# Pairs of chunks in seven block products over all 16 k-tiles, with half of the combined tiles kept in DRAM

## The chip, the cores and the metric

The kernel runs on one core of one Trainium2 chip. The metric is the device time of one execution in microseconds (us); lower is better. TensorE (PE) multiplies, VectorE (DVE), ScalarE (ACT) and GpSimd (POOL) do the element-wise work, SyncE (SP) issues nearly all DMA transfers, in its own order. PSUM is TensorE's output memory, eight banks.

## The reference

Two layers of a hybrid trunk over 640 tokens (128 context, 512 latent) with 2,048 features, in fp32. Each layer normalises, modulates, projects, mixes, gates and projects back:

```python
for l in range(DEPTH):                                    # DEPTH = 2
    shift, scale, gate = modulation(c, ada_w[l], ada_b[l])
    h = rms_norm(x, norm_g[l]) * (1.0 + scale) + shift
    y = even_mixer(h, ...) if l % 2 == 0 else odd_mixer(h, ...)
    x = x + gate * (y @ w_out[l])
y = rms_norm(x, final_norm_g)

def odd_mixer(h, w_in, ...):
    qc, kc, vc, u, v, gp = split_cols(h @ w_in, ODD_SPLITS)   # 48 column blocks of 128 features, and 16 gates
    yc = neighbourhood_attention(qc, kc, vc, ...)             # ctx_attention for context tokens
    yd = spatial_gating(u, v, gnorm, ws, b)
    return jnp.concatenate([yc, yd], -1) * jax.nn.silu(gp)
```

`h @ w_in` and `y @ w_out` are nearly all of the arithmetic. The even layer has its own mixer, which this change leaves as it is.

## The kernel before

Activations lie feature-major: 16 k-tiles of 128 features by 640 token columns, and two leading columns that carry the modulation's shift. A weight chunk is 2,048 input features by 128 output features, so 16 k-tiles by 128. To keep fp32 precision every operand is split into a high part in the fast format fp32r (`ah`, `whi`) and the rest (`al`, `wlo`), and each product is three matmuls: high x high, high weight x low activation, low weight x high activation. The 640 columns are two halves of 320 (322 with the shift columns), one PSUM bank each.

Weights come raw from DRAM (`wraw` for four k-tiles of one chunk, `rs` for block products), ACT makes `whi`, and POOL subtracts it from the raw tile to make `wlo`. `whi` and `wlo` are rings of five blocks of 128x512 (`RING`), filled from a list of jobs (`wstart`, `wpump`).

Most chunks of the first output projection, the odd layer and the second output projection go in pairs (`spair`). Of the 16 k-tiles of two chunks and two column halves, k-tiles 0 to 7 are multiplied plainly and 8 to 15 as a 2 x 2 block product with seven multiplications instead of eight (Strassen's scheme in Winograd's form). With `NS = 4` a block is four k-tiles: weight blocks A11, A12, A21, A22 (`A1x` the first chunk, `x1` k-tiles 8 to 11), their combinations S1 to S4 (DVE block sums, `rs<-rs`), and four combinations of activation tiles. Three of these are kept split in `eh`, `el`; the fourth, T3, overwrites the second column half of k-tiles 8 to 11 in `ah`, `al`. `fold` makes them at a layer's start, and `unfold` reads the overwritten halves back from DRAM (`bh_dram`, `bl_dram`) at its end. Around a fold the chunks run as `kpair`: two chunks k-tile by k-tile, each tile replaced by the next layer's once both have read it.

The raw results of the products meet in PSUM: `sums` holds a copy on ACT, DVE adds it to another bank, and the bank's evacuation follows.

Order: while the program is written out, a planner (`Pace`) estimates when every engine is done with what, and emits an engine's next instruction when it expects its inputs; the engines then run these fixed lists and wait on semaphores. The modulation's matrix-vector work (`adas`, tensor reductions on DVE) fills gaps as the lowest task (`ada_task`). DMA transfers are put on SP's queue when the planner expects them to be free to go. `self.now` is the planner's time.

In the profile L371 is the matmul in `mm`, L376 the transpose in `tr`, L1199 the modulation matmul, L403 the DMA in `dma`, and L205 the one helper line through which DVE, ACT and POOL instructions are recorded, so groups are told apart by tile names.

Of the kernel before, what the change touches and what calls it, by code (L numbers as in the profile page):

```python
# [9 lines left out]
F32 = mybir.dt.float32  # L10
# [16 lines left out]
SPILL, YSP, KEEP = "x1T_dram", "yT_dram", ("bh_dram", "bl_dram")  # L27
# [4 lines left out]
NS = 4  # L32
SJ = KT - 2 * NS
# [5 lines left out]
LAST, STEPS = ((*range(12, 16), *a, *b) for a, b in ((range(8), range(8, 12)), ((*range(4), *range(8, 12)), range(4, 8))))  # L39
LEAD, FIRST = 2, 8  # L40


class Pace:
# [19 lines left out]
    def span(self, ap):  # L63

        if ap.space == bass.MemoryType.DRAM and ap.name not in (SPILL, YSP, *KEEP):
# [165 lines left out]
class Trunk:  # L231
# [9 lines left out]
    def __init__(self, tc, d, es):  # L241
# [11 lines left out]
        self.folded = self.quiet = False  # L253
        self.room = self.rooms[0]
# [11 lines left out]
        self.Y = self.P([128, KT, T], "Y")  # L266
# [29 lines left out]
        self.part = {k: self.P([128, n, 2], "part" + k) for k, n in (("g0", 16), ("1", 32), ("g1", 16))}  # L296


# [12 lines left out]
    def s(self, tag, w=1):  # L311
        return self.t(self.sml, [128, w], tag, bufs=6)
# [74 lines left out]
    cap, hold = 2.0, 99.0  # L387
    lags2, cap2 = (8.0, 6.0, 4.0, 1.0, 0.4), 2.0
    rooms, calms, lags = (0.3, 1.5), (4.0, 2.0), (3.0, 3.0, 2.0, 1.0, 0.4)
# [35 lines left out]
    def until(self, *aps):  # L425
        while self.left(*aps) > 0.05:
# [27 lines left out]
    def tick(self, n=1):  # L454
        self.dmas()
        for _ in range(3):
# [10 lines left out]
        for _ in range(4):  # L467
            if self.low and not (self.quiet and self.tasks) and self.low[0] <= self.now and self.pace.t["v"] <= self.now + self.room:
                try:
                    self.low[0] = max(self.low[0], self.now - 2.0) + (next(self.low[1]) or 0.0)  # L470
                except StopIteration:
                    self.low = None

# [37 lines left out]
    def wstart(self, chunks, acts):  # L511
# [6 lines left out]

        def unit(c, k, r=0):
            self.jobs.append(("split", (c, k, r), len(self.plain), 4, chunks[c][1]))  # L520
            self.plain.append((c, k))
# [4 lines left out]
        last = None  # L526
        self.both = {c for kind, x in acts if kind == "h" for c in x[:2]}
        for kind, x in acts:
# [14 lines left out]
            elif kind == "s":  # L543
                last = self.strassen_jobs(*x, last, unit)

    @staticmethod
    def steps(c1, c2):

        a, b = [[(c, k, 0) for k in range(0, SJ, 4)] for c in (c1, c2)]
        names = lambda *x: [(c1, f) for f in x]  # L550
        return [*names("A11"), *a[:1], *names("A12"), *a[1:], *names("S1", "S2", "S4"), *b[:1], *names("S3"), *b[1:], *names("A22")]

    def strassen_jobs(self, c1, c2, last, unit):
        n, J = NS, self.jobs
        piece = lambda i, m=1: self.rs[:, 128 * n * i : 128 * n * (i + m)]
        load = lambda i, c: ("load", lambda: (piece(i, 2), self.chunks[c][0][:, SJ : SJ + 2 * n, :]))
        add = lambda o, a, b, op: ("add", lambda: (piece(o), piece(a), piece(b)), op)
        if last is None:
            J += [load(0, c1), load(2, c2)]
        else:  # L560
            J.insert(last[0], load(0, c1))
            J.insert(last[1] + 1, load(2, c2))

        at = {"A11": 0, "A12": 1, "S1": 4, "S2": 2, "S4": 1, "S3": 4, "A22": 3}
        after = {
            "A12": [add(4, 2, 3, ALU.add), add(2, 4, 0, ALU.subtract)],
            "S1": [add(1, 1, 2, ALU.subtract)],
            "S2": [add(4, 3, 2, ALU.subtract)],
        }
        for c, f, *r in self.steps(c1, c2):  # L570
            if r:
                unit(c, f)
                continue
            J.append(("split", (c1, f), lambda i=at[f]: piece(i), n, 128))
            J += after.get(f, [])
            if f == "S4":
                done = len(J)
        return done, len(J)
# [4 lines left out]
    def wload(self):  # L583

        c, k = self.plain[self.nraw]
        a = 512 * (self.nraw % 4)
        w = self.chunks[c][0]
        m = w.shape[2]
        self.dma(self.wraws[:, a : a + 4 * m].rearrange("p (a b) -> p a b", b=m), w[:, k : k + 4, :])
# [8 lines left out]
    def wpump(self, force=False):  # L598

        nc, pc = self.nc, self.pace  # L600
        while self.nraw < len(self.plain) and self.nraw < self.nsplit + 4:
# [3 lines left out]
        job = self.jobs[self.job]  # L605
        if job[0] == "load":
            dst, src = job[1]()
            self.dma(dst.rearrange("p (a b) -> p a b", b=128), src)
# [6 lines left out]
            or pc.ready(e, outs, ins) > self.now + lag  # L615
        )
        if job[0] == "add":
            o, a, b = job[1]()
            if not force and late("v", [pc.span(o)], [pc.span(a), pc.span(b)]):
                return False  # L620
            nc.vector.tensor_tensor(o, a, b, job[2])
# [5 lines left out]
        if isinstance(raw, int):  # L627
            m = self.chunks[key[0]][0].shape[2]
            at = 512 * (raw % 4)
# [28 lines left out]
        eng = nc.vector if key[0] in self.both and self.nsplit % 2 else nc.gpsimd  # L658
        eng.tensor_tensor(lo, raw, hi.bitcast(F32), ALU.subtract)
        self.parts[key] = hl  # L660
# [5 lines left out]
    def wget(self, key):  # L666
        while key not in self.parts:
            assert self.wpump(force=True), ("no room for weights", key, self.live)
        return self.parts[key]
# [65 lines left out]
    def kpair(self, c1, c2, order, ready=None, free=None):  # L735
# [7 lines left out]
        for i, (c, k) in enumerate(steps):  # L743
# [3 lines left out]
            if self.folded and SJ <= k < SJ + NS:  # L747
                self.need("unfold")
# [7 lines left out]
            if k == order[-1]:  # L756
                self.chunks[c][4](*banks[c])
# [4 lines left out]
    def hpair(self, c1, c2, after):  # L762

        for half in range(2):
            if half:
                self.need("unfold")
# [14 lines left out]
    def spair(self, c1, c2):  # L781
# [1725 lines left out]
```

## Time and profile before

| | us |
|---|---|
| median of 3 runs (2157.09 to 2159.94) | 2157.79 |
| span of the profiled execution (2.1 below the median; no time of its own beside it is given) | 2155.7 |
| busy: PE / DVE / ACT / POOL | 2099.9 / 1320.2 / 907.2 / 944.9 |
| moved by DMA | 303 MB, 141 GB/s on average |

A group in the profile names engine, operation, output tile <- input tiles with their shape and count, then busy time, mean ns of one, idle time of the engine just before them and what ended it. In a row of waits stand the total, the number and the longest. In an engine's timeline a bracket holds the idle time ahead of an instruction.

### The profile page before, as it was taken

To read this page: it belongs to the slowest core of one execution; us is meant where nothing else is said; L and a number is where in the kernel's file an instruction comes from. 1 tells how busy PE (TensorE), PEld (TensorE's weight loads), DVE (VectorE), ACT (ScalarE), POOL (GpSimd) and SP (SyncE) were. 2 spreads that over 40 slices of the span, in tenths; PEclk is the share of its full clock that TensorE was granted. 3 is DMA by queue.
4 is the path that set the end of the run, shared out by engine and by line. 5 is a ranking of instruction groups with operands and counts; after the bars stand their busy time and mean duration, and the time that the engine had idled before them with its cause. 6 is when DMAs were issued, how large, how long until landed. Compare 5 with 4: busy or idle time off the path is not lost.

```text
span 2155.7 us, 38542 instructions
## 1 busy us (share of the span) xinstructions
PE 2099.9 (97%) x14326; PEld 2029.6 (94%) x14326; DVE 1320.2 (61%) x3190; ACT 907.2 (42%) x1962; POOL 944.9 (44%) x731
## 2 busy tenths in 40 slices
PE   7999999999999999999999999999999999999997
PEld 4789999999989999999999999999999999999996
DVE  1337787777777665889767887874344443354335
ACT  4435444343343444433464333444444453343333
POOL 3433333233223222566544455544444445536663
PEclk9999999999999999999999999999999999999998
DMA  9934433346435332577634345532222232233325
GB/s 374 365 136 153 133 103 105 105 126 192 124 98 165 128 123 81 193 226 220 212 99 127 119 139 163 185 103 79 89 78 78 88 134 80 80 109 122 105 93 193
DMA packets 161372, 303.08 MB, mean 141 GB/s; under 512 B 17376, under 2 KB 54048, under 8 KB 161184
## 3 DMA queue, kind: packets, MB, share of 16 engines
q1 hardware_dynamic: 159712, 299.06, 42.8%
q8 instruction: 112, 1.84, 0.3%
q10 hardware_dynamic: 1472, 1.56, 0.2%
q14 instruction: 76, 0.62, 0.1%
HBM read 278.52 MB, written 19.42 MB: 138 GB/s over the span
## 4 chain that ended last, share of the span: by engine, by line
PE 85%; DVE 5%; DMA 4%; issue 2%; POOL 2%; ACT 2%; SPq 0%; ACTq 0%; DVEq 0%; POOLq 0%
PE bank L371 82%; PE bank L376 2%; PE bank L1199 1%; DVE Y L205 1%; POOL wlo L205 1%; DMA rs<-w_out 1%; DVE arena L205 1%; DVE adas L205 1%; DMA adas<-ada 1%; ACT arena L205 1%; DVE bank L205 0%; ACT whi L205 0%; SPq L403 0%; DVE rs L205 0%; DMA crow<-crow 0%
## 5 line engine op out<-in xcount | busy, mean ns | idle before, releaser
L371 PE MATMUL bank<-acth,whi 128*128 128x320 f32 (+2 forms) x3592 | 1106.6, 318 | 18.2 <-DVE sums L205 8.8
L371 PE MATMUL bank<-acth,wlo 128*128 128x320 f32 (+2 forms) x3592 | 1078.6, 310 | 0.0
L371 PE MATMUL bank<-actl,whi 128*128 128x320 f32 (+2 forms) x3592 | 1077.3, 310 | 0.0
L205 POOL TENSOR_TENSOR wlo<-wraw,whi 128x512 fp32r<-128x512 f32 x375 | 504.2, 1348 | 724.2 <-ACT whi L205 634.0
L371 PEld LDWEIGHTS bank<-acth,whi 128*128 128x128 f32 (+1 forms) x3592 | 668.8, 189 | 35.5 <-DVE sums L205 10.3
L371 PEld LDWEIGHTS bank<-actl,whi 128*128 128x128 f32 (+1 forms) x3592 | 668.9, 189 | 1.5
L371 PEld LDWEIGHTS bank<-acth,wlo 128*128 128x128 f32 (+1 forms) x3592 | 668.4, 189 | 0.0
L205 POOL TENSOR_TENSOR wlo<-rs,whi 128x512 fp32r<-128x512 f32 x259 | 352.1, 1369 | 308.4 <-ACT whi L205 293.0
L205 ACT ACTIVATE whi<-wraw 128x512 fp32r<-128x512 f32 x383 | 237.0, 625 | 251.2 <-PE bank L371 116.0
L205 DVE TENSOR_TENSOR rs<-rs 128x512 f32<-128x512 f32 x148 | 155.2, 1050 | 134.0 <-DMA rs<-w_odd 57.8
L205 DVE CUSTOM_DVE_ANT_0 adas<-adas,bank,partg 128x256 bf16<-128x256 f32 (+1 forms) x320 | 178.6, 558 | 12.7 <-ACT bank L205 3.5
L205 ACT ACTIVATE whi<-rs 128x512 fp32r<-128x512 f32 x259 | 156.4, 621 | 27.3 <-PE bank L371 14.7
L205 DVE CUSTOM_DVE_ANT_0 adas<-adas,bank,part 128x512 bf16<-128x512 f32 x192 | 143.0, 745 | 9.7 <-ACT bank L205 3.6
L205 DVE TENSOR_TENSOR bank<-bank,sums 128x320 f32<-128x320 f32 (+1 forms) x148 | 72.4, 497 | 120.9 <-PE bank L371 120.2
L371 PE MATMUL bank<-eh,whi 128*128 128x322 f32 (+1 forms) x444 | 139.9, 315 | 0.0
L371 PE MATMUL bank<-el,whi 128*128 128x322 f32 (+1 forms) x444 | 137.6, 310 | 0.0
L371 PE MATMUL bank<-eh,wlo 128*128 128x322 f32 (+1 forms) x444 | 137.6, 310 | 0.0
L205 ACT ACTIVATE arena<-Y 128x320 f32<-128x320 f32 (+1 forms) x76 | 38.8, 512 | 172.7 <-DVE Y L205 152.8
L205 ACT ACTIVATE arena<-arena,bc 128x128 f32<-128x128 f32 (+4 forms) x171 | 84.9, 520 | 58.0 <-DVE arena L205 55.8
L205 ACT ACTIVATE bc<-bank 128x2 f32<-128x2 f32 (+1 forms) x101 | 17.2, 170 | 201.1 <-DVE arena L205 120.9
L205 POOL TENSOR_TENSOR arena<-arena 128x320 f32<-128x320 f32 x58 | 53.6, 924 | 103.8 <-ACT arena L205 103.2
L205 ACT ACTIVATE Y<-bank 128x128 f32<-128x128 f32 (+5 forms) x130 | 50.9, 410 | 110.4 <-PE bank L371 85.7
(159 smaller groups left out, 2215.5 us busy)
## 6 DMA issues: line engine op xcount, KB each, us to landing
wraw<-w_even SPq DMA_DIRECT2D x176, 256.0 KB, 3.2
adas<-ada_g SPq DMA_DIRECT2D x128, 256.0 KB, 3.7
adas<-ada SPq DMA_DIRECT2D x128, 256.0 KB, 3.6
wraw<-w_odd SPq DMA_DIRECT2D x124, 256.0 KB, 3.1
rs<-w_odd SPq DMA_DIRECT2D x50, 512.0 KB, 4.1
wraw<-w_out SPq DMA_DIRECT2D x88, 256.0 KB, 3.3
Y<-ada SPq DMA_DIRECT2D x37, 512.0 KB, 6.9
more<-ada SPq DMA_DIRECT2D x27, 512.0 KB, 7.1
```

The source lines that it names most:

```text
L205: return f(*args, **kw)
L371: self.nc.tensor.matmul(out, lhsT, rhs, start=start, stop=stop, **kw)
L376: self.nc.tensor.transpose(out, in_, self.ident[:k, :k])
L1199: nc.tensor.matmul(o, c, w[:, j, :], start=(q == 0), stop=(q == 3))
```

## The change

`NS` becomes 8: a full pair takes all 16 k-tiles in seven block products of eight tiles, as two halves of four (`h` = 0 near, 1 far), and has no plain part. Nine of the 37 pairs keep the form before (`ns = NR = 4`), with blocks of four k-tiles and a plain part: all six of the first output projection, one in the odd layer and the first two of the second projection (`SHORT`).

```diff
-NS = 4
-SJ = KT - 2 * NS
+NS = 8
+NR = 4
+SHORT = 6, 2
 ...
+    def steps(c1, c2, ns):
+        if ns == NS:
+            todo = "A11' A11 S1' S1 A12 A12' S4 S2' S2 S4' S3 S3' A22' A22".split()
+            return [(c1, f.rstrip("'"), int(f[-1] == "'")) for f in todo]
 ...
-        at = {"A11": 0, "A12": 1, "S1": 4, "S2": 2, "S4": 1, "S3": 4, "A22": 3}
+        at = {"11": 0, "21": 1, "22": 2, "12": 3}
+            sums = {
+                "S1": ("21", "21", "22", ALU.add),
+                "S2": ("11", "21", "11", ALU.subtract),
+                "S4": ("12", "12", "11", ALU.subtract),
+                "S3": ("21", "22", "11", ALU.subtract),
+            }
 ...
+        dve = self.nsplit % 2 if key[0] in self.both else self.share and pc.t["g"] > max(pc.t["v"], self.now) + self.share
+        if dve and self.share:
+            self.lows.append((key, hl[0], lambda: (sub(nc.vector), self.parts.update({key: hl})), raw))
 ...
+    def far_load(self, i, f, shift):
+        o = 0 if shift else 2
+        self.dma(self.slots[i][:, :, o:].bitcast(U32), self.far[:, i, f, :, o:].bitcast(U32))
 ...
+            for i in range(4):
+                three(view(b), hi[:, i, :], lo[:, i, :], x(4 * key[2] + i), st and i == 0, i == 3)
+                if again is not None and key[2]:
+                    self.far_load(i, again, shift)
 ...
+                yield from sub(j1, j2, j1)
+                yield from sub(j2, m2, j2)
+                yield from split(self.t3[:, i], self.stage, j2)
+                yield from sub(m2, m2, j1)
+                yield from split(out(0), j2, j1)
+                yield from sub(m1, m1, m2)
+                yield from split(out(1), self.stage, m2)
+                yield from split(out(2), j1, m1)
 ...
+                for n, x in enumerate((self.ah, self.al)):
+                    self.dma(x[:, i, CW:].bitcast(U32), self.t3[:, i, n, :].bitcast(U32))
 ...
-        for j in range(SJ, SJ + NS):
+        for j in range(self.deep):
             for x, y in zip((self.ah, self.al), self.keep):
-                self.dma(x[:, j, CW:].bitcast(U32), y[:, j - SJ, :].bitcast(U32))
+                self.dma(x[:, j, CW:].bitcast(U32), y[:, j, :].bitcast(U32))
 ...
-                    pairs((KT - 4) // 2)
+                    pairs((KT - 4) // 2, SHORT[l], f"us{l}")
```

What comes with it:

- The combined tiles of the near half stay in `eh`, `el`. Those of the far half are made on POOL by `far` (eight subtractions of 320 columns for each of four tile pairs), stored to DRAM (`far_dram`), and streamed into four slots of a tile `tail`. A slot is loaded with the next combination when its product has read it.
- To make room, `Y`, the store of mixer outputs, has 12 tiles of its own instead of 16; four more lie in `tail` while it holds no slots, two borrow the modulation's buffer `adas` (`GHOSTS`), and parts of the attention's and the gating unit's results pass through DRAM (`hT_dram`, `yT_dram`).
- T3 is made for all eight near and far tiles at the fold, stored (`t3_dram`) and read into `ah`, `al` (`third`); `unfold` returns up to eight column halves instead of four.
- Raw weight blocks are 128x1024 and use `rs` and `wraw` together. A low part goes to DVE where the planner sees POOL more than 1 us behind (`share`).
- Bank evacuations and pieces of `fold` are handed out when the planner expects their data (`defer`, `settle`) and no longer stand in an engine's list ahead of it.
- The modulation for the odd layer is fetched as scale, then shift, and the scaling of its input runs as a task (`scales`).

SP's queue beside two attention heads of the odd layer. `rs` and `wraw` are raw weights, `o_nv`, `na_bias` and the caches belong to the attention, `tail<-far_dram` is a load of a far slot, `ada_g` a modulation weight. Before:

```order
L403 DMA rs_7718<-w_odd 128x1024
L403 DMA wraw<-w_odd 128x512 x2
L403 DMA Y<-na_bias 128x1024
L403 DMA Y<-cache_na_kT 128x128
L403 DMA Y<-cache_na_v 128x128
L403 DMA o_nv<-Y 128x128
```

Now:

```order
L428 DMA tail_10968<-far_dram 128x644 x4
L428 DMA adas<-ada_g 128x2x256
L428 DMA hT_dram<-Y 128x640
L428 DMA o_nv<-Y 128x128
L428 DMA Y<-na_bias 128x1024
L428 DMA Y<-cache_na_kT 128x128
L428 DMA Y<-cache_na_v 128x128
L428 DMA tail_10968<-far_dram 128x644 x4
L428 DMA wraw<-w_odd 128x1024
```

The far loads, four at a time, have come into the one queue between weights, modulation weights and the attention's own transfers.

POOL over one pair of the second output projection. `wlo` is a low part of the weights, `arena<-arena` the square of a new output. Before:

```order
L205 TENSOR_TENSOR wlo<-rs_7718,whi 128x512
L205 TENSOR_TENSOR wlo<-wraw,whi 128x512
L205 TENSOR_TENSOR wlo<-rs_7718,whi 128x512
L205 TENSOR_TENSOR wlo<-wraw,whi 128x512
L205 TENSOR_TENSOR arena_16766<-arena_16766 128x320 x2
L205 TENSOR_TENSOR wlo<-rs_7718,whi 128x512 x3
L205 TENSOR_TENSOR wlo<-wraw,whi 128x512
L205 TENSOR_TENSOR arena_16766<-arena_16766 128x320
L205 TENSOR_TENSOR wlo<-rs_7718,whi 128x512
L205 TENSOR_TENSOR wlo<-wraw,whi 128x512
L205 TENSOR_TENSOR wlo<-rs_7718,whi 128x512
L205 TENSOR_TENSOR arena_16766<-arena_16766 128x320
```

Now:

```order
L208 TENSOR_TENSOR arena_16792<-arena_16792 128x320 x2
L208 TENSOR_TENSOR wlo<-rs_7767,whi 128x512 x4
L208 TENSOR_TENSOR wlo<-wraw,whi 128x512 x2
L208 TENSOR_TENSOR arena_16792<-arena_16792 128x320
L208 TENSOR_TENSOR wlo<-wraw,whi 128x512 x2
L208 TENSOR_TENSOR wlo<-rs_7767,whi 128x512
L208 TENSOR_TENSOR arena_16792<-arena_16792 128x320
L208 TENSOR_TENSOR wlo<-rs_7767,whi 128x512 x3
L208 TENSOR_TENSOR wlo<-wraw,whi 128x512
```

The pair had 11 low parts between its four squares; it now has 13 on POOL, and a fourteenth on DVE.

More of the change, by code (lines that the diff above doesn't have):

```diff
@@ new lines, in later, with one, two, three_ @@
+        def later(c, gen):
+            self.evq.append([self.now, gen, c])
+        def one(xa, x):
+            yield from self.until(x)
+            plus(full(xa), x)
+            yield from ev(c1, xa, None)
+            self.drop(xa)
+        def two(x, v):
+            yield from self.until(x)
+            plus(x, half(v))
+        def three_(xb, x):
+            yield from self.until(x)
+            plus(half(xb), x)
+            yield from ev(c1, None, half(xb))
+            self.drop(xb)
@@ new lines, in four @@
+        def four(ya, v, x):
+            yield from self.until(x)
+            plus(full(ya), x)
+            plus(half(v), half(x))
+            yield from ev(c2, ya, None)
+            yield
+            yield from ev(c2, None, half(v))
+            self.drop(ya, v)
+        t = take()
+        xa = xb = v = ya = None
+        steps = self.steps(c1, c2, ns)
+        for n, key in enumerate(steps):
+            c, f, h = key
+            last = f not in [x[1] for x in steps[n + 1 :]]
+            if isinstance(f, int):
+                if c == c1:
+                    xa, xb = xa or take(), xb or take()
+                    plain(key, xa, xb)
+                else:
+                    ya = ya or take()
+                    plain(key, ya, v)
+                if c == c1 and f > NS:
+                    later(c1, one(xa, x))
@@ L865, in spair @@
-                ev1(xa, None)
-                self.drop(xa)
-                v = take()
-                product(v, full, f, tt(0))
+                if v is None:
+                    v = take()
+                    self.need("Tf" if ns == NS else "Tn")
+                product(v, full, key, tt(0), 1)
             elif f == "S2":
-                product(t, full, f, tt(1))
-                x = copy(half(t))
-                plus(x, half(v))
+                product(t, full, key, tt(1), 2)
+                if last:
+                    x = copy(half(t))
+                    later(c1, two(x, v))
@@ L898, in fold @@
+                if last:
+                    later(c2, four(ya, v, x))
+    def fold(self, ready, used, far_used, shift=None, yt=None):
+        nc = self.nc
+        yt = yt or (lambda k: self.Y[:, k, :])
+        self.flags -= {"Tn", "Tf", "T30", "T31"}
+        if not far_used:
+            self.flags |= {f"{ready}f{k}" for i in range(NR, NS) for k in (i, NS + i)}
         one, two = slice(0, HT), slice(HT, T)
         left = [2, 2]
+        staged = []
+        pair = lambda x: x.rearrange("p (a b) -> p a b", b=HT)
@@ L952, in fold @@
+        if shift is not None:
+            self.spawn(shifts())
         for w in range(2):
             self.spawn(work(w))
+        if far_used:
+            self.spawn(far(0))
+            self.spawn(far(1))
+        self.spawn(third())
     def split2(self, h, l, x, scale=1.0):
@@ L1686, in evac, with end @@
             G = self.G[l]
-            y = self.Y[:, f, :]
+            y = self.yt(f) if l else self.Y[:, f, :]
+            if l == 0 and f in GHOSTS:
+                y = box["x"]
+            def end(c):
+                yield from self.until(y[:, c], self.sq)
+                square(y, c)
+                if c.start and spill is not None:
+                    self.dma(spill[:, f, :], y)
+                    self.flags.add(f"sp{f}")
+            x = box["x"]
             if pa is not None:
-                x = box["x"]
+                self.need(f"y{l}f{f}")
                 nc.vector.scalar_tensor_tensor(
```

685 lines of the change are left out of this document (464 added, 221 removed).

## The prediction

> **What bounds the kernel now.** I read the page's head first, then busy time by stage, then who makes TensorE wait, then single instructions in the stages that the change rewrites.
>
> The head of the page, engine and busy time:
>
> ```profile
> span 2155.7 us, 38542 instructions
> PE 2099.9 (97%) x14326; PEld 2029.6 (94%) x14326; DVE 1320.2 (61%) x3190; ACT 907.2 (42%) x1962; POOL 944.9 (44%) x731
> L371 PE MATMUL bank<-acth,whi 128*128 128x320 f32 (+2 forms) x3592 | 1106.6, 318 | 18.2 <-DVE sums L205 8.8
> ```
>
> TensorE is busy 97% of the span, but matmuls overlap: 318 ns is the life of one, not what one costs. The price is the distance of two starts, from TensorE's timeline (start, duration, instruction); the two rows are 28 matmuls apart in an unbroken run:
>
> ```profile
> 1299.75 0.31 PE L371 MATMUL bank<-acth,whi 128*128 128x320 f32 x1
> ...
> 1303.89 0.31 PE L371 MATMUL bank<-el,whi 128*128 128x322 f32 x1
> ```
>
> (1303.89 - 1299.75) / 28 = 0.148 us per matmul of 320 or 322 columns. By stage (first number the length, then busy time and count of PE, PEld, DVE, ACT and POOL, the granted clock, DMA share, GB/s):
>
> ```profile
> 900.00:1050.00 150.00, 142.20 (x958) 140.92 (x958) 128.82 (x313) 49.46 (x102) 97.66 (x82) 1.00 0.72 225
> 1050.00:1200.00 150.00, 147.00 (x985) 145.74 (x985) 101.00 (x271) 79.44 (x186) 68.21 (x53) 0.99 0.45 139
> 1200.00:1400.00 200.00, 200.00 (x1378) 199.93 (x1377) 163.85 (x459) 77.31 (x162) 105.36 (x78) 1.00 0.47 148
> 1400.00:1760.00 360.00, 359.03 (x2385) 345.79 (x2385) 172.42 (x500) 157.01 (x366) 158.83 (x122) 1.00 0.27 85
> 1760.00:1930.00 170.00, 168.71 (x1140) 168.30 (x1140) 67.96 (x109) 71.98 (x146) 83.92 (x63) 1.00 0.32 105
> 1930.00:2156.00 226.00, 210.53 (x1421) 209.19 (x1419) 101.45 (x180) 84.09 (x165) 136.16 (x112) 0.97 0.38 127
> ```
>
> The first output projection is 900 to 1050, the odd layer about 1050 to 1930, the second output projection and the end come last. From 1050 to 1930 TensorE idles 5.3 us of 880 and its clock is full: there a matmul less is 0.148 us less, as long as its operands arrive. DVE, ACT and POOL have room in that stage; DVE is nearest to full at 1200 to 1400 with 164 of 200 us.
>
> **The change, part by part.** *Matmuls removed.* A pair of chunks costs 96 + 7 x 4 x 3 = 180 matmuls before (eight plain k-tiles in two chunks and two halves, three matmuls each, and seven products of four tiles), and 7 x 8 x 3 = 168 now. Of the 37 pairs nine keep the short form (six in the first output projection, one in the odd layer, two in the second projection), so 28 x 12 = 336 go, all of them after 1050 us. The built order agrees: 13,534 matmul rows before, 13,198 now, no other kind changed in sum. 336 x 0.148 = **49.7 us** less, the gain if TensorE stays fed.
>
> *Splitting and adding weights.* A full pair splits 14 half blocks in place of 11 and adds 8 in place of 4. The order has 726 high parts on ACT in place of 642 (84 x 0.62 = 52 us on an engine that is 42% busy: nothing); low parts 623 on POOL and 112 on DVE in place of 643 and 8; block sums 260 on DVE in place of 148; and 64 new subtractions of 320 columns on POOL. What these cost depends on one another, as the timelines show (POOL at two places, then DVE at the same):
>
> ```profile
> 1811.30 1.29 POOL L205 TENSOR_TENSOR wlo<-wraw,whi 128x512 fp32r<-128x512 f32 x1 [1.61 <-DVE bank L205]
> 1816.93 4.30 POOL L205 TENSOR_TENSOR wlo<-rs,whi 128x512 fp32r<-128x512 f32 x3 [4.34 <-ACT whi L205]
> ...
> 963.39 0.88 POOL L205 TENSOR_TENSOR arena<-arena 128x320 f32<-128x320 f32 x1 [0.60 <-ACT arena L205]
> 968.72 1.84 POOL L205 TENSOR_TENSOR wlo<-wraw,whi 128x512 fp32r<-128x512 f32 x1 [0.70 <-ACT whi L205]
> ...
> 1816.45 0.69 DVE L205 TENSOR_TENSOR rs<-rs 128x512 f32<-128x512 f32 x1
> 1818.32 1.76 DVE L205 TENSOR_TENSOR rs<-rs 128x512 f32<-128x512 f32 x1 [1.19 <-POOL wlo L205]
> ...
> 968.71 2.40 DVE L205 TENSOR_TENSOR rs<-rs 128x512 f32<-128x512 f32 x2 [1.35 <-DMA rs<-w_out]
> ```
>
> A block sum takes 0.69 us where POOL has only just begun, and 1.76 us inside POOL's run of 4.30: it stood for 1.07 us. POOL's own 1.29 becomes 1.84 at 968.72, beside two block sums that began at 968.71. So DVE's two-input work and POOL's take turns, and their times add up against TensorE's.
>
> In the second projection the order has, over the 660 matmuls of its full pairs (97.7 us), 50 low parts and 16 squares on POOL, and 28 sums and 6 low parts on DVE: 50 x 1.29 + 16 x 0.88 + 34 x 0.69 = 64.5 + 14.1 + 23.5 = 102 us. That is 4 us more than TensorE needs. Bounds: 0, if low parts made ahead and the short pairs' slack cover it; 18, if each of the 34 also holds POOL up by 0.55 (1.84 against 1.29) on top. I take **+4**, nearest to the free durations. For the odd layer I need the length of its full pairs, by the first and the last combined-tile products there (duration in ns least/median/most, first and last start):
>
> ```profile
> L371 PE MATMUL bank<-eh,whi x20: 307/311/314, 1157.5 to 1189.4; 128*128 128x322 f32 x20
> L371 PE MATMUL bank<-eh,whi x4: 309/312/314, 1890.2 to 1891.6; 128*128 128x322 f32 x4
> ```
>
> From the second pair's start (1157.5 + 26.6 for a pair - 10.7 for the 72 matmuls ahead of this product = 1173) to 1892 it is 719 us for 24 pairs, and 719 - 288 x 0.148 = 676 now. POOL's and DVE's turns there are 278 x 1.29 + 247 x 0.69 = 529 us: 78%, hidden, 0.
>
> The Trainium skill speaks against the change here ("SBUF — State Buffer", section "Who interferes with whom"): a DVE instruction with two SBUF inputs and a GpSimd instruction that reads SBUF exclude each other for the whole instruction, and the second is blocked, not slowed. The trace agrees (1.76 against 0.69). By a bandwidth that is merely shared the term would be 0; by the lock it is the 4 above or more.
>
> *The far tiles.* Each full pair streams three sets of four combined tiles (330 KB each) from DRAM into four slots: a slot is loaded again when its product has read it, and used 58, 58 and 46 matmuls later: 8.6, 8.6 and 6.8 us. The trace has no such load. The nearest: 320 KB reads, 512 KB and 256 KB weights over the whole run, then in the busiest steady stretch, then 320 KB in the saturated first 90 us (KB each, median us from issue to landing):
>
> ```profile
> rs<-w_out SPq DMA_DIRECT2D x24, 512.0 KB, 4.3
> wraw<-w_out SPq DMA_DIRECT2D x88, 256.0 KB, 3.3
> ```
> ```profile
> wraw<-w_out SPq DMA_DIRECT2D x23, 256.0 KB, 4.3
> rs<-w_out SPq DMA_DIRECT2D x9, 512.0 KB, 5.5
> arena<-xT SPq DMA_DIRECT2D x10, 320.0 KB, 3.8
> ```
> ```profile
> GB/s 10 294 174 418 419 417 397 391 404 408 411 402 380 401 413 408 400 406 409 396 407 403 403 406 402 402 324 338 355 412 339 383 409 412 374 392 334 349 273 340
> Y<-xT SPq DMA_DIRECT2D x13, 320.0 KB, 7.6
> ```
>
> A full pair moves 2.1 MB of weights and 12 x 0.33 = 4.0 MB of tiles in 168 x 0.148 = 24.9 us: 244 GB/s, near the 225 of 900 to 1050, against some 400 at full rate. One load lands in 3.8 us; the fourth of a set queues 3 x (0.33/0.4 - 0.44) = 1.2 us behind the others, 5.0; at this load the weights land 1.0 to 1.2 us later than on average, so 6.2. Against 6.8 that holds on medians, but only by 0.6 us. Bounds: 0, and 28 us if every pair loses 1 us in its tight gap. I take a late load of 0.5 us in a third of the 28 tight gaps, **+5**.
>
> *SP's queue* now carries 1,497 transfers in place of 1,064, in order, and weight loads stand at its head until POOL has read their buffer:
>
> ```profile
> SPq L403 <- POOL wlo L205: 1267.7, 402, 13.9
> SPq L403 <- DVE partg L205: 88.7, 55, 6.1
> ```
>
> 402 waits of 3.2 us on average cost nothing so far, since only weights for later lay behind them. A far tile behind such a wait is late by it; the bounds above hold this too.
>
> *Hand-overs.* Before the first full pair of a layer the four far tile pairs are combined on POOL (32 x 0.88 = 28 us per layer), stored and loaded; the fourth combination of all tiles (T3) now goes through DRAM; at a layer's end eight column halves come back instead of four. In the odd layer the far combination has one k-pair and the short pair to finish: 192 + 180 + 24 matmuls, 58.6 us, for 28 us of far work and 8 + 11 + 4 low parts, 30 us if all are POOL's. That just fits. The returning halves are needed some 36 matmuls (5.3 us) after the last pair, against these rows:
>
> ```profile
> acth<-bh_dram SPq DMA_DIRECT2D x12, 160.0 KB, 4.4
> actl<-bl_dram SPq DMA_DIRECT2D x12, 160.0 KB, 4.8
> ```
>
> Bounds 0 and 12 (three hand-overs of one landing, 4 us each); I take **+4**.
>
> *The rest.* The first projection keeps its short pairs; of its 7.8 idle us most is this:
>
> ```profile
> PE bank L371 <- DVE sums L205: 7.8, 5, 2.3
> ```
>
> Evictions are now handed out when their data is there, which may win up to 4 of these; the modulation work on DVE is partly drawn forward and may cost as much. I take 0. The modulation fill otherwise stays in the gaps DVE has.
>
> Sum: -49.7 + 4 + 5 + 4 = -36.7 on a span of 2155.7. The profile gives no time of its own around that span; the median of the runs is 2157.8, 2.1 above it, and I keep this distance: 2157.8 - 36.7 = **2121**.
>
> **Rivals.** *All is hidden:* the four terms are 0 as the order was laid for it; 2108, or 2104 with the 4 us of the first projection. For it: 5.3 idle us in 880. Against it: the 102 us in 98.
>
> *The shared turns bind in every full pair:* this is the lock named above, as a result of its own. The rows' means instead of the free durations:
>
> ```profile
> L205 POOL TENSOR_TENSOR wlo<-rs,whi 128x512 fp32r<-128x512 f32 x259 | 352.1, 1369 | 308.4 <-ACT whi L205 293.0
> L205 DVE TENSOR_TENSOR rs<-rs 128x512 f32<-128x512 f32 x148 | 155.2, 1050 | 134.0 <-DMA rs<-w_odd 57.8
> ```
>
> 50 x 1.37 + 16 x 0.92 + 34 x 1.05 = 119 against 97.7: +21 in the second projection; the odd layer's 278 x 1.37 + 247 x 1.05 = 640 of 676 us would just hold. With +21 in place of +4 the time is 2138, and 2145 if the odd layer loses 1%.
>
> *Far tiles come late in every pair: slower.* If DMA saturates at 1200 to 1400, where the modulation weights are fetched beside them, a 320 KB load lands in 7.6 us and the fourth in 8.8: 0.2 + 0.2 + 2.0 = 2.4 us lost per pair, 67 us; 2121 - 5 + 67 = 2183. It decides from 1.5 us lost per pair ((49.7 - 8) / 28). For it: SP's waits of 3.2 us. Against it: 244 of 400 GB/s.
>
> *Nothing gained:* about half of that lateness, 40 us, and 2156.
>
> **Chances.** Forecast (2112 to 2132) 0.50; all hidden 0.15; turns bind 0.18; nothing gained 0.06; slower 0.11. The range goes from 2104 to 2150: it leaves out the slower case and most of "nothing gained". The likeliest case alone has 2112 to 2132. Faster by over 0.2% (4.3 us, about what a measurement can tell): 0.50 + 0.15 + 0.18 and a third of the sixth case, 0.85; within 0.2%, 0.04; slower, 0.11.
>
> **What would show it.** Right: 13,198 matmuls of the same 0.148 us; from 1050 on TensorE idles some 13 us more; POOL and DVE together are full in the second projection, DVE's sums there at 1.0 us or more. Far loads land in 4 to 6 us; waits of TensorE for DMA on the tail tile add to about 5. Wrong: TensorE waits for tail loads in every pair, or for low parts through the whole odd layer, or DMA near its full share there.

## The result, and the profile after

The changed kernel is slower: 2185.9 us median (2180.7 to 2190.5, four runs) against 2157.7 for the kernel before, a ratio of 1.013 (95% interval 1.0112 to 1.0147). The forecast was 2121, in a range of 2104 to 2150. It was to become 37 us faster and became 28 us slower.

The head of the page after, engine and busy time, and its row for the far tiles' loads (KB each, median us to landing):

```profile
span 2185.5 us, 39032 instructions
PE 2083.0 (95%) x13990; PEld 1992.6 (91%) x13990; DVE 1537.5 (70%) x3389; ACT 959.0 (44%) x2084; POOL 1021.9 (47%) x775
...
tail<-far_dram SPq DMA_DIRECT2D x288, 322.0 KB, 4.8
```

14,326 - 13,990 = 336 matmuls are gone, as forecast, and in an unbroken run they still start 0.148 us apart. DVE is busy 217 us more. By stage, in the columns of the table of before:

```profile
900.00:1050.00 150.00, 149.17 (x1010) 148.27 (x1009) 125.28 (x310) 62.17 (x126) 87.46 (x72) 1.00 0.67 215
1050.00:1200.00 150.00, 137.55 (x887) 133.40 (x886) 90.19 (x193) 72.71 (x171) 77.54 (x66) 0.97 0.65 205
1200.00:1400.00 200.00, 190.80 (x1267) 186.27 (x1266) 161.88 (x331) 81.55 (x177) 113.55 (x80) 0.98 0.74 251
1400.00:1760.00 360.00, 345.77 (x2215) 324.57 (x2214) 281.50 (x775) 171.21 (x401) 174.75 (x128) 0.99 0.70 238
1760.00:1930.00 170.00, 166.02 (x1099) 163.90 (x1099) 118.53 (x155) 79.39 (x165) 105.06 (x73) 0.99 0.68 236
1930.00:2186.00 256.00, 224.02 (x1469) 219.67 (x1467) 151.26 (x217) 102.71 (x203) 172.23 (x139) 0.95 0.69 229
```

The first projection is better than before (1,010 matmuls in place of 958, and TensorE is never long idle). Every stage behind it makes fewer matmuls per microsecond: 4,369 in place of 4,748 from 1050 to 1760. The granted clock there is below 1, and DVE in 1400 to 1760 is busy 282 us in place of 172. What TensorE waits for from 1060 on (us in total, times, longest), of after:

```profile
PE bank L394 <- DMA tail<-far_dram: 11.1, 9, 4.2
PE bank L394 <- ACT whi L208: 9.9, 7, 3.2
PE bank L394 <- POOL wlo L208: 7.2, 9, 1.4
PE bank L394 <- ACT Y L208: 4.1, 2, 3.7
```

and the longest row of the same view of before:

```profile
PE bank L371 <- DVE Y L205: 2.4, 1, 2.4
```

There is no one new wait but many kinds of short ones. I followed the distances of matmul starts from 1050 to 2050: gaps over 0.4 us, less the 0.148 that a matmul costs, sum to 71 us in place of 11. The far tiles are late in nine places, not in every pair. In the others a weight, a returning half, an evacuation or a step of attention on ACT or DVE is late. One of them in full, the stall of 2.13 us at 1552.7, from the timelines of PE, of ACT and of DVE of after (start, duration; idle before, and releaser, in brackets):

```profile
1552.72 0.57 PE L394 MATMUL bank<-tail,whi 128*128 128x322 f32 x2 [2.13 <-ACT whi L208]
```
```profile
1550.59 0.56 ACT L208 ACTIVATE arena<-arena,nm 128x320 f32<-128x320 f32 x1 [1.35 <-DVE nm L208]
...
1552.06 1.14 ACT L208 ACTIVATE whi<-rs 128x512 fp32r<-128x512 f32 x2
```
```profile
1546.09 0.69 DVE L208 TENSOR_TENSOR wraw<-rs,wraw 128x512 f32<-128x512 f32 x1
...
1550.41 0.15 DVE L208 TENSOR_SCALAR nm<-mx 128x1 f32<-128x1 f32 x1
```

TensorE waits for a high part. ACT could have made it earlier, but its list has attention's exponential ahead of it, and that waited for a maximum (`nm`) which DVE reached late, behind sums and scalings of its own list. So a delay on DVE passes through ACT's order to a weight that has nothing to do with it. The sums in this piece of DVE's list run at 0.69 us, the length they have alone: this stall shows how a list passes a delay on, and not the exclusion of DVE and POOL. In before such a delay stayed hidden: following each of the ring's blocks from the end of its low part to its first matmul, the median lead from 1173 to 1750 was 7.1 us in the first part of that stretch and 8.4 in the second (5 in 100 below 3.1 and 6.2); after it is 3.4 and 3.1 (5 in 100 below 0.5 and 0.15).

### The profile page after: what moved, and what is told of

It is laid out like the page before. It is cut to its first block, busy times and chain, and to the rows that moved or that the text cites. A ratio compares the mean times of both kernels' runs of the same rounds, so it can differ in the third digit from the quotient of the medians.

```text
span 2185.5 us, 39032 instructions
## 1 busy us (share of the span) xinstructions
PE 2083.0 (95%) x13990; PEld 1992.6 (91%) x13990; DVE 1537.5 (70%) x3389; ACT 959.0 (44%) x2084; POOL 1021.9 (47%) x775
## 4 chain that ended last, share of the span: by engine, by line
PE 67%; DMA 11%; DVE 10%; issue 5%; POOL 3%; ACT 3%; SPq 1%; ACTq 0%; POOLq 0%; DVEq 0%
PE bank L394 64%; DMA tail<-far_dram 2%; POOL wlo L208 2%; DVE arena L208 2%; DVE Y L208 2%; PE bank L399 2%; DVE adas L208 1%; PE bank L1510 1%; DMA rs<-w_odd 1%; DVE bank L208 1%; SPq L428 1%; DMA wraw<-w_odd 1%; DMA adas<-ada_g 1%; DVE wlo L208 1%; DVE actl L208 1%
## 5 line engine op out<-in xcount | busy, mean ns | idle before, releaser
L394 PE MATMUL bank<-acth,whi 128*128 128x320 f32 (+1 forms) x3144 | 968.4, 319 | 24.5 <-DMA acth<-bh_dram 6.5
L394 PE MATMUL bank<-acth,wlo 128*128 128x320 f32 (+1 forms) x3144 | 942.4, 311 | 4.9 <-POOL wlo L208 3.2
L394 PE MATMUL bank<-actl,whi 128*128 128x320 f32 (+1 forms) x3144 | 941.0, 311 | 1.5 <-DMA actl<-bl_dram 1.5
L394 PEld LDWEIGHTS bank<-acth,whi 128*128 128x128 f32 x3144 | 586.1, 189 | 44.1 <-ACT whi L208 7.3
L394 PEld LDWEIGHTS bank<-acth,wlo 128*128 128x128 f32 x3144 | 585.0, 189 | 7.9 <-POOL wlo L208 5.1
L394 PEld LDWEIGHTS bank<-actl,whi 128*128 128x128 f32 x3144 | 586.2, 189 | 3.4 <-DMA actl<-bl_dram 1.9
L208 ACT ACTIVATE whi<-wraw 128x512 fp32r<-128x512 f32 (+1 forms) x429 | 261.7, 623 | 166.6 <-PE bank L394 94.7
L394 PE MATMUL bank<-tail,whi 128*128 128x322 f32 (+1 forms) x672 | 159.2, 323 | 16.4 <-DMA tail<-far_dram 11.1
L394 PEld LDWEIGHTS bank<-tail,whi 128*128 128x128 f32 x672 | 112.8, 192 | 25.0 <-DMA tail<-far_dram 16.5
L394 PE MATMUL bank<-tail,wlo 128*128 128x322 f32 (+1 forms) x336 | 105.7, 315 | 3.5 <-POOL wlo L208 3.5
```

The source lines that it names most:

```text
L208: return f(*args, **kw)
L394: self.nc.tensor.matmul(out, lhsT, rhs, start=start, stop=stop, **kw)
```

## The experiments

All edits are to the changed kernel unless said otherwise. Where an edit only shortens an instruction, the order of all instructions is the same. The changed kernel stands at 2186, before at 2156 to 2158 in each group.

**1. What carries the loss: bytes, element-wise work, the rest of the change, or the order.**

```diff
 # far tiles small: all far loads after a layer's first set
-        self.dma(self.slots[i][:, :, o:], self.far[:, i, f, :, o:])
+        self.dma(self.slots[i][:, 0, o : o + 128], self.far[:, i, f, 0, o : o + 128])
```

> The changed kernel in the same order, but the loads of combined tiles (all after a layer's first set) move 128 x 128 floats each instead of 128 x 2 x 322, 64 KB in place of 330 KB, about 88 MB less; the products of combined tiles then read tiles left over from earlier, which no time depends on. Traffic theory (the bytes of the far tiles make weights, halves and tiles late): the waits on the tail tile (11 us) and most of the late weights and returning halves (27 us) go, and the half-clock windows behind them (11 us): 2135 to 2150. Turns theory (DVE and POOL exclude each other, low parts are late whatever DMA carries): only the tail waits and a few windows go, 2168 to 2180. Order theory (places at which the order itself leaves no slack): 2170 to 2186.

2173.2 us (ratio to before 1.0081, 1.0063 to 1.0098): 13 us less. The bytes count, but are not the loss.

```diff
 # sums and low parts small
-            nc.vector.tensor_tensor(o, a, b, job[2])
+            nc.vector.tensor_tensor(o[:, :64], a[:, :64], b[:, :64], job[2])
-        sub = lambda e: e.tensor_tensor(lo, raw, hi, ALU.subtract)
+        sub = lambda e: e.tensor_tensor(lo[:, 0, :64], raw[:, 0, :64], hi[:, 0, :64], ALU.subtract)
```

> The changed kernel in the same order, but the block sums on DVE and the low-part subtractions (on POOL and DVE, from the first output projection on) write only 64 columns of their 512; what they leave out is left stale in the low parts and sums. Turns theory: waits for low parts and sums, high parts that wait behind them, and attention's late evacuation go, about 35 us with the windows behind them: 2140 to 2155; what stays are waits for DMA. Traffic theory: the weights are late at their landing, so at most 10 us go: 2172 to 2186. Order theory: 2165 to 2186.

2139.4 us (0.9921, 0.9905 to 0.9938): 46 us less, just beyond what the turns theory had. The cut also shortens sums and low parts that the kernel before has as well. The same cut was not made there, where all gaps from 1050 to 2050 sum to 11 us, so a part of the 46, at most about 11, may not be the change's own.

```diff
 # all pairs short
-(c[2 * i], c[2 * i + 1], NR if i < short else NS, used if i == short - 1 else None)
+(c[2 * i], c[2 * i + 1], NR, None)
```

> All pairs keep seven products of four k-tiles and eight plain ones (336 matmuls more, 49.7 us), so no far tile is stored or loaded and only 11 blocks are split a pair; the rest of the change (deferred evacuations, the split stores, T3 through DRAM, the new placing of weight loads) stays. If full pairs make the stalls (traffic or turns): back to the kernel before or a little faster by the better first projection, 2148 to 2160. If the rest of the change makes them: 49.7 us of matmuls on top of stalls that stay, 2190 to 2236.

2162.5 us (1.0029, 1.0017 to 1.0040). So the full pairs make the stalls. The rest of the change costs 6 us at the same number of matmuls; most of it is one wait of 4.7 us for the first returning halves at 1063.

```diff
 # planner: later landings
-            pc.note("q", o, i, pc.t["d"] + 1.0)
+            pc.note("q", o, i, pc.t["d"] + (2.4 if self.share else 1.0))
```

> The changed kernel with one number of the planner other: it assumes that a load lands 2.4 us after its transfer's modelled end instead of 1.0 us, from the first output projection on; work and result are the same, the order is laid out for later landings. If stalls come because the order puts readers ahead of data that is late (in-order engines then block on it): 2150 to 2172. If the lateness is made of bytes or of turns, the order can't help: 2180 to 2195.

2180.2 us (1.0105, 1.0087 to 1.0122); the interval overlaps the changed kernel's. Planning for later landings does not take the loss away. A second rule of the order, how long before its data are due a split or sum may be placed, was tried later:

```diff
-            self.share, self.soon = 1.0, 0.6
+            self.share, self.soon = 1.0, 3.0
```

> The changed kernel with one rule of the planner as it was before: a split or block sum may be placed up to 3 us before its data are due (the change set 0.6 us). Same work, another order. If the rule is what cut the lead of the weights: 2160 to 2176. If the lead is cut by the ring and by the low parts' length: 2180 to 2192.

2184.9 us (1.0132, 1.0105 to 1.0160): no difference that can be told.

**2. Which side of the element-wise work.** The two cuts of the second run, one at a time:

> The changed kernel in the same order, with only DVE's block sums cut to 64 of 512 columns (what they leave out is stale); low parts stay whole. Cutting sums and low parts together gave 2139. If what hurts is that the two exclude each other (each must wait for the other's whole instruction), taking away either side takes most of it: 2145 to 2160. If it is the length of the low parts alone (POOL at 1.4 us each behind its high part): 2170 to 2183.

> The changed kernel in the same order, with only the low-part subtractions (POOL's and DVE's, after the first projection's start) cut to 64 of 512 columns; block sums stay whole. Exclusion: 2145 to 2160, as with the sums cut, since DVE's sums then run free at 0.69 us. Low parts alone: nearly all of it, 2139 to 2148. DVE's length of queue alone (its sums and evictions in order): 2160 to 2175.

Sums small: 2165.4 us (1.0040, 1.0027 to 1.0053), 20 us less. Low parts small: 2139.0 us (0.9917, 0.9899 to 0.9934), 47 us less, all that the two together gave. The first is just below what "the length of the low parts alone" allowed and above what exclusion was to give, and the second lies at the edge of what the low parts alone would give, below the range for exclusion. So this pair alone doesn't decide. The rows show the exclusion itself. DVE's block sums from 1173 to 1890 of after, with low parts small, and with sums themselves small (busy, mean ns):

```profile
L208 DVE TENSOR_TENSOR rs<-rs 128x512 f32<-128x512 f32 x54 | 55.0, 1031 | 16.7 <-POOL wlo L208 11.3 <-DMA rs<-w_odd 5.0
```
```profile
L208 DVE TENSOR_TENSOR rs<-rs 128x512 f32<-128x512 f32 x54 | 37.7, 705 | 13.6 <-DMA rs<-w_odd 7.2 <-POOL wlo L800 6.1
```
```profile
L758 DVE TENSOR_TENSOR rs<-rs 128x64 f32<-128x64 f32 x54 | 28.8, 544 | 18.8 <-POOL wlo L208 16.6 <-DMA rs<-w_odd 2.0
```

Beside small low parts a whole sum takes 0.70 us instead of 1.03. Beside whole low parts a sum of 64 columns takes 0.54, and with both small it takes 0.22:

```profile
L758 DVE TENSOR_TENSOR rs<-rs 128x64 f32<-128x64 f32 x54 | 11.7, 225 | 18.1 <-POOL wlo L801 12.0 <-DMA rs<-w_odd 5.4 <-issue 0.6
```

Whoever comes second stands still. What was open was whether that costs the time, or simply the length of DVE's list:

```diff
 # block sums replaced by a reduction: nearly as long, one SBUF operand
-            nc.vector.tensor_tensor(o, a, b, job[2])
+            nc.vector.tensor_reduce(o[:, :1], a, AX.X, ALU.add)
```

> The changed kernel in the same order, with each of DVE's block sums replaced by a sum along one block's 512 columns into one column: one operand in SBUF instead of two, at 512/960 + 0.1 = 0.63 us nearly the 0.69 that a sum takes alone (estimates from the sums' 0.70 us with the low parts cut); the sums left out are stale. If the two-input sums and POOL's low parts hurt by excluding each other: as with the sums cut short, 2160 to 2172, with these instructions at 0.6 to 0.7 us and low parts at 1.3 us. If the length of DVE's queue hurts: 2180 to 2188.

2167.0 us (1.0042, 1.0026 to 1.0058), as with the sums cut to 64 columns. The instructions keep 0.68 us, and POOL's low parts fall from 1.41 to 1.33:

```profile
L758 DVE TENSOR_REDUCE rs<-rs 128x1 f32<-128x512 f32 x84 | 56.5, 679 | 17.1 <-POOL wlo L208 16.7
...
L208 POOL TENSOR_TENSOR wlo<-rs,whi 128x512 fp32r<-128x512 f32 x168 | 220.9, 1325 | 205.4 <-ACT whi L208 156.3 <-PE bank L394 15.0 <-DVE partg L208 6.4
```

So it is the second operand, not the 0.68 us: about 19 us of the loss are exclusion between the sums and POOL (the reduction also no longer waits for the second block's load, which was not separated). The remaining 28 that the small low parts gave are their own length and their exclusion with DVE's other work; these two are not separated.

The modulation's products read one operand from PSUM and keep 0.48 us in every kernel; they were cut by themselves:

```diff
-nc.vector.tensor_tensor_reduce(junk, raw[:, k, :], bank[c], ...)
+nc.vector.tensor_tensor_reduce(junk[:, :16], raw[:, k, :16], bank[c][:, :16], ...)
```

> The changed kernel in the same order, with DVE's modulation products (multiply and reduce, one operand in PSUM, 0.48 us each, about 220 of them in the odd layer) cut to 16 of 256 columns; their sums are then not the reference's. They keep POOL from nothing. If DVE's in-order queue is what is full (it is busy 40 of 50 us until the fill ends near 1750, and the stretch behind that has no stall): 2150 to 2168. If only the exclusion counts: 2176 to 2186.

2178.5 us (1.0106, 1.0081 to 1.0131): 7 us at most, and the interval meets the changed kernel's. Shortening some 220 of DVE's instructions that exclude nobody wins little.

**3. The lead of the weights.** The ring held to four half blocks instead of five, in both kernels:

```diff
             a = self.space(n * M)
-            if a is None:
+            if a is None or len(self.live) >= 4 and hasattr(self, "rs") and key[0] not in self.both:
```

> The kernel before, with the ring of split weights held to four live half blocks of four k-tiles instead of five (from the first output projection's setup on); same work. Lead theory: five half blocks of before cover 5 x 180/11 = 82 matmuls (12.1 us), four cover 65 (9.7 us), and the full pairs of the change cover 5 x 12 = 60 (8.9 us); if that short lead is what lets a late evacuation or sum through to TensorE, this kernel stalls too: 2175 to 2200. Turns theory (the stalls come of DVE and POOL being fuller, not of the lead): 2155 to 2164.

> The changed kernel with four live half blocks instead of five: 48 matmuls (7.1 us) of cover instead of 60 (8.9 us). Lead theory: much slower, 2220 to 2270. Turns theory: a little, 2186 to 2205.

Before: 2165.0 us (1.0042, 1.0025 to 1.0059), 9 us more, with three new stalls of 0.85 to 1.4 us in its profile. After: 2208.7 (1.0243, 1.0228 to 1.0259), 23 more. Both lie between the two theories' ranges. A short lead by itself does not stall the kernel before much, and it costs the changed kernel more; that it does so by making other delays visible is a reading and was not tested.

**4. The second projection, the hand-over, and whether causes add.**

```diff
-SHORT = 6, 2
+SHORT = 6, 6
```

> The changed kernel with the second output projection's pairs all in the short form (48 matmuls more, 7.1 us), the odd layer as changed. From the traces: from the odd layer's end to the end of the span it is 274 us with four full pairs, and 259 us in the run in which all pairs were short. If the stalls there belong to that projection's full pairs and their hand-over: 2186 - 15 = 2171. If they are carried in from the odd layer: 2186 + 7 = 2193.

2171.2 us (1.0074, 1.0045 to 1.0102), the 15 us expected: the four full pairs of that projection, with their hand-over, cost more than their 7.1 us.

```diff
 # POOL's combining of the far tiles small
-                nc.gpsimd.tensor_tensor(o, x, y, ALU.subtract)
+                nc.gpsimd.tensor_tensor(o[:, :64], x[:, :64], y[:, :64], ALU.subtract)
```

> The changed kernel in the same order, with POOL's 64 subtractions that combine the far tiles (0.88 us each, 28 us per hand-over) cut to 64 of 320 columns; the combined tiles are stale. If the hand-over's element-wise work makes the stalls between 1060 and 1210 and behind 1910: 2166 to 2176. If those stalls come of the returning halves and of attention's start: 2180 to 2187.

2173.0 us (1.0081, 1.0057 to 1.0104): 13 us less. The order is the same, so the two profiles can be compared matmul by matmul. They differ by 19 us behind 1050: 5 come between 1050 and 1200 and 6 between 2000 and 2050, around the two hand-overs, but 7 between 1200 and 1930, where POOL combines nothing. How those 7 come about stays open.

Small far loads, sums and low parts in one kernel:

> The changed kernel in the same order with the far loads at 64 KB, and sums and low parts at 64 columns, together (what they leave out is stale). If bytes and turns are separate causes their gains add: 2186 - 46 - 13 = 2127. If both act through the same shortage of lead, little is left for the bytes: 2133 to 2140. The matmuls alone would allow 2108.

2127.7 us (0.9864, 0.9843 to 0.9884), against 2127 for a plain sum: bytes and element-wise work are separate losses. From the landing of the first projection's first returning half to that of the odd layer's first it is 836.1 us in before, 853.1 us in after, 834.0 with small far loads, 818.7 with small low parts, 807.0 with all small, and 839.8 with all pairs short. 288 matmuls less than the last would be 797.

**5. Full pairs only where they did not stall, and a way out.** The pairs given a second number are short that many times; the second projection is short as well.

```diff
-        pairs(2, 1, "us2")
+        pairs(2, 2)
-        pairs(4)
+        pairs(4, 4)
-        pairs(13)
+        pairs(13, 13, "us2")
```

> The changed kernel with full pairs only in the odd layer's last six (the gates, behind attention and the modulation fill); all other pairs short, in the second projection too. In the changed kernel the stretch from 1800 to 1900 has full pairs and no stall. Against the run with all pairs short (2162) 6 x 12 x 0.148 = 10.7 us go: 2150 to 2154. If full pairs always pay their gain back, or the far tiles' hand-over costs as much: 2158 to 2170.

2175.4 us (1.0095, 1.0073 to 1.0118), against the 2150 to 2154 expected; this order computes a part of the latent tokens' output wrongly, and which step does so was not found; number and size of its instructions are as planned. A miss: 13 us slower than all short. Its hand-over, still at 1050 to 1200, has 876 matmuls where the kernel with all pairs short has 957 (12 us), and the first full pair starts with waits of 1.8 and 0.8 us for far tiles at 1770. Six full pairs don't pay for a hand-over.

Then the exclusion itself, taken away by giving the low parts to the engine that does the sums:

```diff
 # who takes a low part: DVE, when POOL is later than DVE by self.share
-            self.share, self.soon = 1.0, 0.6
+            self.share, self.soon = -99.0, 0.6     # the next: -0.6
```

> The changed kernel with one rule of the planner other: from the first output projection on every low part that the changed rule could give to DVE goes there (544 on DVE and 182 on POOL, in place of 112 and 614); same work. DVE and POOL then hardly meet: a low part takes 0.69 us in place of 1.4, and sums 0.70 in place of 1.03. DVE's busy time from 1060 to 1910 would go from 634 to about 634 - 110 + 280 x 0.69 = 717 of 850 us. If the exclusion is what counts and a queue of 84% can still serve in time: 2145 to 2170, and a way to keep the change. If DVE's order then holds up evictions and attention: 2190 to 2230.

> As the changed kernel, with DVE taking a low part wherever POOL is less than 0.6 us ahead of it, not only when POOL is over 1 us behind (177 low parts on DVE and 549 on POOL, in place of 112 and 614). 65 low parts then take 0.69 us of the shared turns in place of 1.3: 40 us of turns less in all. Exclusion: 2172 to 2182. DVE's queue: 2186 to 2196.

All on DVE: 2176.8 us (1.0106, 1.0079 to 1.0132); again a part of the latent tokens' output is computed wrongly, with as many matmuls, high and low parts as in the changed kernel. A balance of 177: 2173.1 (1.0071, 1.0050 to 1.0093), the 40 us of turns less being worth 13. The first one's stages show why it misses (1050 to 1760, columns as above):

```profile
1050.00:1200.00 150.00, 120.86 (x750) 116.37 (x749) 83.47 (x183) 63.55 (x151) 38.94 (x38) 0.91 0.57 183
1200.00:1400.00 200.00, 197.10 (x1339) 195.48 (x1339) 186.70 (x447) 86.91 (x183) 3.46 (x2) 0.99 0.78 265
1400.00:1760.00 360.00, 353.50 (x2316) 336.67 (x2314) 304.75 (x859) 175.71 (x415) 4.23 (x3) 0.99 0.72 240
```

DVE is busy 187 of 200 us, and TensorE makes 1,339 matmuls in place of 1,267 there. But in the hand-over it makes 750 in place of 887. The two longest rows of TensorE's waits there, from 1050 to 1200:

```profile
PE bank L399 <- ACT Y L208: 7.0, 4, 4.3
PE bank L394 <- ACT acth L208: 6.5, 1, 6.5
```

`acth` is the odd layer's own input. ACT had waited 1.78 us for DVE (`part`) ahead of it, and DVE's list up to there holds low parts and modulation products. No wait for a combined tile is among the rows, and how much of the 137 matmuls the low parts on DVE account for was not separated. So the last kernel switches the rule on behind the hand-over and off at the odd layer's last full pair, with the second projection short:

```diff
+        do(lambda: setattr(self, "share", -99.0))   # behind the odd layer's second pair
+        do(lambda: setattr(self, "share", 1.0))     # behind its last full pair
```

> Made of the pieces that the runs point to: the second output projection's pairs all short (2171 alone), and every low part that may go to DVE goes there only inside the odd layer, from behind its hand-over to its last full pair; in the hand-over (where the run with all low parts on DVE lost 137 matmuls of 150 us) the changed kernel's balance stays. In that run 1200 to 1930 held 4772 matmuls against 4581, 28 us more work done. If the exclusion was the loss in the full pairs and DVE's queue can carry the rest: 2171 - 28 = 2143 (2138 to 2152), faster than the kernel before. If what was won there is given back at the layer's ends: 2158 to 2172.

2150.1 us (five runs, 2146.8 to 2153.1; ratio 0.9960, 0.9946 to 0.9973): faster than both kernels, by 8 and 36 us, inside what was expected. Of the 36, the second projection's short pairs alone had given 15 (2171.2); the switch gives the other 21. In its odd layer POOL does 25 low parts, and DVE's instructions run at their free length:

```profile
L208 DVE TENSOR_TENSOR wlo<-rs,whi 128x512 fp32r<-128x512 f32 x187 | 129.3, 701 | 23.2 <-ACT whi L208 22.6
...
L208 DVE TENSOR_TENSOR rs<-rs 128x512 f32<-128x512 f32 x54 | 37.0, 687 | 0.7
```

Its odd layer takes 828.0 us between the same two points, in place of 853.1, and of 836.1 before. So of the 42.6 us that 288 matmuls less are worth there (288 x 0.148) it keeps 8. Here a busier DVE that is alone on its operands beats two engines in turns.

## Why the prediction was wrong, step by step

*Matmuls removed, -49.7:* right in number and price. But the gaps between matmuls from 1050 to 2050 grew by 60 us, where the text expected TensorE to idle some 13 us more.

*Splitting and adding weights, +4:* the step that failed. Low parts at 64 columns give 47 us back, 34 of them in the odd layer (853.1 to 818.7), where the text said "78%, hidden, 0"; some 10 more come behind it, where the +4 stood. The exclusion itself was seen, and the rival priced it with nearly the durations that came (1.37 us for a low part and 1.05 for a sum; 1.41 and 1.03 in the odd layer after). What was wrong is the test: the sum of the turns was held against TensorE's time, as if work that fits on average were hidden. The engines' lists are in order, attention's steps on ACT and DVE stand between the weights, and a low part has to be done before its block's first matmul, with the ring's five half blocks (60 matmuls, 8.9 us) as all the store ahead, not somewhere in a pair's 25 us. That the lists pass delays on was followed for one stall alone; of the 47 us the 19 of the sums' exclusion are shown to be that, and how the other 28 divide stays open. The sum also left out DVE's other instructions that stand still beside POOL, and all that waits behind them. The rival "shared turns bind in every full pair" named the mechanism, but let the odd layer lose 1% of 676 us; 34 came back there. Two slips carry no term of the sum: the low parts on POOL are 634 and 614 in the traces, not 643 and 623, and 34 x 0.55 = 18.7 "on top" of the 4 is a bound of 23, not 18.

*Far tiles, +5:* 13 measured, inside its bounds of 0 to 28, but for the most part not where the text looked. The fourth load of a set landed in 5.3 us on the median, where 6.2 was estimated. Of the nine waits (11.1 us) only two, 1.1 us in all, are in the tight gap; three, 5.7 us, are at the second projection's first full pair; the other four are in the wider gaps, the longest of these (2.34 us at 1354) in a stretch where DMA moved 356 GB/s and not the 244 of the text. That the size fell inside the bounds is partly luck. The rival with late tiles in every pair gave 2183, the right time by a mechanism that is not there.

*Hand-overs, +4 of at most 12:* about 13 with POOL's combining cut, of which the profiles place 11 around the hand-overs; and the first halves return 4.3 us late (a wait that the kernel with all pairs short has as well). "That just fits" was again a comparison of sums.

*The rest, 0:* 6 us by the kernel with all pairs short.

-49.7 + 46 + 13 + 13 + 6 = +28, the measured difference. Of these only that bytes and turns add was shown; that the hand-over's 13 and the rest's 6 don't overlap with them was not, so that the sum comes out exactly is in part luck.

*Not in the prediction at all:* "its clock is full" was taken over from before. After a stall the clock is halved for a while. The stretch before, in and behind such a window (granted clock is the third number from the end):

```profile
1352.10:1355.50 3.40, 0.72 (x4) 0.45 (x3) 3.40 (x5) 0.00 (x0) 1.89 (x2) 1.00 1.02 356
1355.50:1358.90 3.40, 3.21 (x12) 3.21 (x13) 0.04 (x1) 0.63 (x1) 1.27 (x1) 0.50 1.03 376
1358.90:1362.30 3.40, 3.40 (x25) 3.40 (x24) 2.15 (x7) 1.18 (x4) 0.38 (x1) 1.00 0.73 277
```

A wait of 2.34 us at 1352 leaves TensorE busy 0.72 of 3.4 us, and the next 3.4 us run at half clock: 12 matmuls, 0.27 us apart, where 3.4 / 0.148 = 23 fit. That loses up to 11 x 0.148 = 1.6 us. Twelve such windows lie between 1050 and 2050, one in before; by the matmul starts in all that come behind 1050 they cost 12 us in place of 1. That is inside the losses above. By these numbers a window adds about half to the price of a stall of 2 to 4 us (an estimate), and it was in no term of the sum. The Trainium skill ("TensorE: Matmul & The Clock Gate", section "Part 1: The HAM clock gate") has the halved clock and a window of about 3.4 us; it asks for a whole idle window, while here one with 0.72 us of work was enough, and the measurement decides.

## What to carry to other kernels

Work that fits into an engine's time on average is not hidden: ask how long ahead of its use each piece is finished, and what stands between in the in-order lists. Where two engines exclude each other, the second instruction stands still and delays whatever is queued behind it; giving both jobs to the engine that does them faster can win even where it fills that engine, as long as no stage with its own deadline runs beside it. A change that saves matmuls should have its stalls priced with the half-clock window behind them.

## What the runs showed of the hardware that was not expected

Not only DVE's sums with two SBUF operands stand still beside POOL. Attention's scaling, one SBUF operand and a scalar for each partition, does too (from 1173 to 1890, after and with sums and low parts small):

```profile
L208 DVE TENSOR_SCALAR Y<-Y,den 128x320 f32<-128x320 f32 (+2 forms) x30 | 19.8, 660 | 1.1
```
```profile
L208 DVE TENSOR_SCALAR Y<-Y,den 128x320 f32<-128x320 f32 (+2 forms) x30 | 11.7, 389 | 1.1
```

while the reduction of one operand kept 0.68 us and products with one operand in PSUM 0.48. The Trainium skill ("SBUF — State Buffer", section "Who interferes with whom") lists `tensor_scalar` among the operations that can take the shared pair of ports, and `tensor_reduce` as one that never does on this chip; both agree. The prediction cited this section for sums alone. Counting such rows in the profile of before (attention's scaling was at 507 there, above its free 389) would have shown that more of DVE's list than the sums was already slowed.
